# Four of seven w_down operands with their low part by DMA, and a later start of VectorE's larger planned cost

## The chip, the cores and the metric

The kernel runs on one core of a Trainium2 chip. The metric is the device time of one execution in microseconds (us), lower is better; the time of a version is the median of several runs. Engines: TensorE (PE, with PEld for its weight loads), VectorE (DVE), ScalarE (ACT), GpSimd (POOL) and SyncE (SP), which issues most of the DMAs.

## The reference, cut to what matters

One step of a hybrid decoder layer for 1032 tokens (1024 prompt and 8 sample tokens), width 1024, in float32. The part that matters here is the end of the layer:

```python
x = x + cross_attn(rmsnorm(x, g_attn), mk, mv, w_q, w_o)
h = rmsnorm(x, g_ffn)
x = x + (jax.nn.silu(h @ w_gate) * (h @ w_up)) @ w_down     # D_FF = 2816
y = rmsnorm(x, g_final)
```

## The kernel before

**Precision.** Every float32 operand of a product is split into a high part (float32 rounded to TensorE's float32r format, written by a copy) and a low part (the operand minus its high part). A product is three passes, high by high, high by low and low by high (`PASSES`, line 53). Two helpers make the parts. `split` (line 338) has the high part written by ScalarE or GpSimd and the low part by a subtraction on VectorE or GpSimd. `split_by_dma` (line 363) has ScalarE write the high part (line 368), then minus the high part into the low part's place (line 368 again, `hb<-hb`), and then GpSimd's queue issues a DMA that adds the raw operand from DRAM to it (line 375, `hb<-hb`, an accumulating DMA).

**The gate and up products.** 22 tiles of 128 hidden columns, in a Strassen-like scheme with seven products a tile (`of_tokens`, `product` at line 1273, matmuls at line 1290) in place of eight; VectorE adds the products from PSUM into `su` (line 1305), VectorE or GpSimd multiply by the row factor `Rf` (line 1331), ScalarE takes the silu (line 1338). The weights of a tile are added up (line 1249) and split (lines 346 to 357) into `wG`, `wU`, `wTa`, `wTb` while the tile before runs. The first 16 tiles leave their hidden values, already combined to seven operands, in DRAM (`hb`), in four chunks of 512 rows of w_down; the last six go through `hd` and the stage after.

**The w_down products.** 4 chunks of 4 units (`down(u)`, chunk c = u // 4), each of seven products (`A11, S2, A12, S3, S1, A22, S4`, the order of `DOWN_ORDER`, line 57). A unit's weights are loaded (`dn_load`, `dr`), added up (`dn_prep`, line 1431, `dt`) and split into `dW` and `dV`, one unit ahead. The chunk's seven operands are loaded by SP (`down_blocks`, tile `hs`) and split into `hb` tiles: chunk 0 by `split`, chunks 1 to 3 by `split_by_dma` (line 1449). They are asked for during the chunk before, two in its second unit, two in its third and three (S1, A22, S4) in its fourth. In chunk 0 four results of a unit go out of PSUM by ScalarE (line 1309), all the others by VectorE (line 1305). After the 16 units `last_down` (line 1587) takes the last six tiles, and the final norm follows.

**The order of the work.** Nothing is ordered by hand here. `Program.add` notes each piece of work with its planned cost on every engine that may take it, its reads and its writes; `Program.order` then plans all pieces at once, always the one that can start first, with small slacks and a priority by place in the program, and emits the instructions in that order. So the planned costs decide which engine gets a piece and in which order each engine's queue runs; the chip then runs each queue in order. VectorE's planned cost is `dve(n) = fixed["DVE"] + 0.00105 * n`, with a fixed part of 0.065 at the start of the program and 0.148 from the attention output projection on (line 1512). It is read when a piece is noted. In the plan GpSimd does not start while a VectorE piece marked `lock` runs, nor the other way round; on the chip no wait between the two is emitted for that. Tiles come from small pools: 19 of the big operand tiles (`op`), 3 `scr` (among them `hs`), 3 `raw` (`dr`, `dt`), and in PSUM `mm` and `ms`, which hold three products at a time.

Of the kernel before, what the change touches and what calls it, by code (L numbers as in the profile page):

```python
# [66 lines left out]
DOWN_ORDER = (A11, S2, A12, S3, S1, A22, S4)  # L67
# [175 lines left out]
def hybrid_step_kernel(ctx: ExitStack, tc: tile.TileContext, io):  # L243
# [11 lines left out]
    def buf(name, tag, shape, dtype=F32):  # L255
        return Buf(name, tag, shape, dtype)
# [4 lines left out]
    def op_r(name, shape=(P, 2, T)):  # L261
        return buf(name, "op", shape, F32R)

    def scr(name, shape=(P, T)):
        return buf(name, "scr", shape)
# [20 lines left out]
    fixed = {"DVE": 0.065}  # L286
# [47 lines left out]
    def dma(out, in_, nbytes, r=(), w=()):  # L334

        add({"SP": 0.05}, lambda e: e.dma_start(out(), in_()), r, w, nbytes=nbytes)

    def split(dst, key, src, n, r, gain=None, ps=False):

        hi = {"ACT": act(n, ps, gain is not None)}  # L340
        if not ps:
            hi["Pool"] = pool_ts(n)

        def emit_hi(e):
            if e is nc.scalar:
                e.activation(dst(0), src(), AF.Copy, scale=1.0 if gain is None else gain)
            else:
                e.tensor_scalar(dst(0), src(), 1.0 if gain is None else gain, 1.0, ALU.mult, ALU.mult)

        add(hi, emit_hi, r, [key(0)])  # L350
        lo = {"DVE": dve(n)}
        if gain is None and not ps:
            lo["Pool"] = pool_tt(n)

        def emit_lo(e):
            if gain is None:
                e.tensor_tensor(dst(1), src(), f32(dst(0)), ALU.subtract)  # L357
            else:
                e.scalar_tensor_tensor(dst(1), src(), gain, f32(dst(0)), ALU.mult, ALU.subtract)

        add(lo, emit_lo, list(r) + [key(0)], [key(1)], lock=not ps)

    def split_by_dma(dst, key, src, n, r, again, again_keys, pool_too=False):


        def scaled(e, p, src, factor):
            if e is nc.scalar:
                e.activation(dst(p), src, AF.Copy, scale=factor)  # L368
            else:
                e.tensor_scalar(dst(p), src, factor, 1.0, ALU.mult, ALU.mult)  # L370

        either = {"ACT": act(n), "Pool": pool_ts(n)} if pool_too else {"ACT": act(n)}
        add(either, lambda e: scaled(e, 0, src(), 1.0), r, [key(0)])
        add(either, lambda e: scaled(e, 1, f32(dst(0)), -1.0), [key(0)], [key(1)])
        add({"Pool": 1.04}, lambda e: e.dma_start(dst(1), again(), accum_op=ALU.add), [key(1)] + again_keys, [key(1)], nbytes=4 * P * n)
# [848 lines left out]
    def gu_load(f):  # L1224
        gu_raw[f] = [buf(f"gr{f}_{i}", "raw", (P, D)) for i in range(2)]
        for i, raw in enumerate(gu_raw[f]):
            dma(lambda raw=raw: raw[:], lambda i=i: io["w_gu"][2 * f + i], 4 * P * D, w=[(raw,)])
# [4 lines left out]
    def gate_prep(f):  # L1232
        rg, _ = gu_raw[f]
        gu_w[f] = [buf(f"wG{f}", "w", (P, 2, 1024), F32R)]
        parts(gu_w[f][0], lambda: rg[:], 1024, [(rg,)])

    def sums_prep(f):
        rg, ru = gu_raw.pop(f)
        U = buf(f"wU{f}", "w", (P, 2, 512), F32R)
        Ta, Tb = op_r(f"wTa{f}", (P, 2, 1024)), op_r(f"wTb{f}", (P, 2, 1024))  # L1240
        ta, tb = scr(f"ta{f}", (P, 1024)), scr(f"tb{f}", (P, 1024))
        gu_w[f] += U, Ta, Tb
        lo, hi = slice(0, 512), slice(512, 1024)

        def minus(dst, sl, a, asl, b, bsl, op=ALU.subtract):
            def key(t, s):
                return (t,) if t in (rg, ru) else (t, s.start)

            add({"Pool": pool_tt(512), "DVE": dve(512)}, lambda e: e.tensor_tensor(dst[:, sl], a[:, asl], b[:, bsl], op),
                [key(a, asl), key(b, bsl)], [key(dst, sl)], lock=True)  # L1250

        minus(tb, lo, ru, lo, rg, lo)
        minus(ta, lo, tb, lo, ru, hi)
        minus(ta, hi, ru, hi, ru, lo)
        minus(tb, hi, rg, hi, ta, lo, ALU.add)
        parts(Ta, lambda: ta[:], 1024, [(ta, 0), (ta, 512)])
        parts(Tb, lambda: tb[:], 1024, [(tb, 0), (tb, 512)])
        parts(U, lambda: ru[:, hi], 512, [(ru,)])
# [97 lines left out]
    def first_two(f, between=lambda: None):  # L1356
        G = gu_w[f][0]
        su[f] = op_buf(f"su{f}", (P, 4, TH))
        copy_sums(part(f, 1), (su[f], 1), of_tokens(G, 0, A11, 4 if f < AHEAD else 1))
        between()  # L1360
        plus(f, 1, 0, of_tokens(G, 512, A12, 4 if f < AHEAD else 1))
        gated(f, 0)

    def sixth(f):
        plus(f, 1, 2, of_tokens(gu_w[f][2], 0, S2, 4 if not f else 1))
# [30 lines left out]
    def later(work, bias="prep"):  # L1396
        pg.later = BIAS[bias]
        work()
        pg.later = 0
# [15 lines left out]
    def dn_load(u):  # L1415
        dn_raw[u] = buf(f"dr{u}", "raw", (P, D))
        dma(lambda: dn_raw[u][:], lambda: io["w_dn"][u], 4 * P * D, w=[(dn_raw[u],)])

    def dn_prep(u):
        raw, t = dn_raw[u], buf(f"dt{u}", "raw", (P, D))  # L1420
        W, V = buf(f"dW{u}", "w", (P, 2, 768), F32R), op_r(f"dV{u}", (P, 2, 1024))
        dn_w[u] = W, V

        def b(half, i):
            return lambda: raw[:].rearrange("p (k i n) -> p k i n", k=4, i=2)[:, half::2, i]

        def s(q):
            return lambda: t[:].rearrange("p (q j n) -> p q j n", q=4, j=2)[:, q]

        def minus(q, a, b, keys, op=ALU.subtract):  # L1430
            add({"Pool": pool_tt(256), "DVE": dve(256)}, lambda e: e.tensor_tensor(s(q)(), a(), b(), op), keys, [(t, q)], lock=True)

        minus(0, b(0, 1), b(0, 0), [(raw,)])
        minus(2, s(0), b(1, 1), [(raw,), (t, 0)])
        minus(3, b(1, 1), b(0, 1), [(raw,)])
        minus(1, b(1, 0), s(2), [(raw,), (t, 2)], ALU.add)
        split(lambda p: V[:, p], lambda p: (V, p), lambda: t[:], 1024, [(t, q) for q in range(4)])
        split(lambda p: W[:, p, :512].rearrange("p (k n) -> p k n", k=4), lambda p: (W, p, 0),
              lambda: raw[:].rearrange("p (k i n) -> p k i n", k=4, i=2)[:, :, 0], 512, [(raw,)])
        split(lambda p: W[:, p, 512:].rearrange("p (k n) -> p k n", k=2), lambda p: (W, p, 1), b(1, 1), 256, [(raw,)])  # L1440

    def down_blocks(c, which):
        for b in which:
            t = scr(f"hs{c}_{b}", (P, 2, TH))
            dma(lambda t=t: t[:], lambda b=b: hb[c, b], 8 * P * TH, r=[("hb", c, b, j) for j in range(2)], w=[(t,)])
            o = db[c, b] = op_r(f"hb{c}_{b}", (P, 2, 2, TH))
            part, key, src = (lambda p, o=o: o[:, p]), (lambda p, o=o: (o, p)), (lambda t=t: t[:])
            if c:
                split_by_dma(part, key, src, T, [(t,)], lambda b=b: hb[c, b], [("hb", c, b, j) for j in range(2)])
            else:  # L1450
                split(part, key, src, T, [(t,)])
# [57 lines left out]
        hops.append(ho)  # L1509


    fixed["DVE"] = 0.148
    for n in O_ORDER:
        proj_o(n)
        j, i = n % 4, n // 4
# [14 lines left out]
    for f in range(FF_TILES):  # L1530
        if f + 1 < FF_TILES:
            if f + 1 >= AHEAD:
                later(lambda: gu_load(f + 1), "load")
                later(lambda: gate_prep(f + 1))
            later(lambda: sums_prep(f + 1))
        else:
            later(lambda: dn_load(0), "load")
            later(lambda: dn_prep(0))
            later(lambda: down_blocks(0, DOWN_ORDER[:4]))
        if f < AHEAD:  # L1540
            sixth(f)
        else:
            first_two(f, lambda: sixth(f))
        others(f)
    later(lambda: down_blocks(0, DOWN_ORDER[4:]))
    units = 4 * CHUNKS
    for u in range(units):
        c, p = u // 4, u % 4
# [191 lines left out]
```

## Time and profile before

| | before |
|---|---|
| median of 3 runs | 1266.01 us (1265.66 to 1266.23) |
| the profiled execution | 1266.04 us, of it span 1264.2 us |
| busy: PE, PEld | 1218.6 us (96%), 1196.0 us (95%) |
| busy: DVE, ACT, POOL | 909.9 us (72%), 531.8 us (42%), 497.8 us (39%) |
| mean granted TensorE clock | 0.991 |
| gate and up products | 556.43 to 1010.48 us of the span |
| w_down products, 16 units | 1010.48 to 1182.26 us |
| last six tiles, final norm | 1182.26 us to the end |

An engine's row in the timeline gives the start, the time and the count of merged instructions; the bracket behind it is the idle time of the engine just before and what ended it. The chain of waits follows the work that ended last back through what released each step. Below, "stall" is idle time of TensorE.

### The profile page before, as it was taken

What the parts mean: (1) busy time and instruction counts of PE and PEld (TensorE: products, weight loads), DVE (VectorE), ACT (ScalarE), POOL (GpSimd) and SP (SyncE); (2) the same over time, 40 slices, a digit from 0 to 9 for tenths busy, and PEclk for the clock granted to TensorE, in tenths of its full rate; (3) what the DMA queues carried; (4) which work ended last, traced back from release to release, by engine and by line L of the source; (5) the groups of instructions that cost most, each with busy time, mean ns of one, the idle gap of its engine ahead of it and who ended that gap; (6) DMA issues with size and microseconds to landing.
All of it is one profiled execution on the core that took longest, in us unless ns stands there. A gap on an engine that the chain in (4) does not pass through costs nothing.

```text
span 1264.2 us, 22138 instructions
## 1 busy us (share of the span) xinstructions
PE 1218.6 (96%) x8958; PEld 1196.0 (95%) x8958; DVE 909.9 (72%) x1542; ACT 531.8 (42%) x733; POOL 497.8 (39%) x436
## 2 busy tenths in 40 slices
PE   8999997999999999999999999999999999999996
PEld 7999986999999889989999999999999989999996
DVE  7899888667367786578776868686766767766644
ACT  6766658454233443453222222222222355533544
POOL 3578741032101112125353334334433558768401
PEclk9999997999999999999999999999999999999998
DMA  7447696644265663231333133313313598889703
GB/s 278 104 83 167 144 248 171 204 106 158 89 220 198 233 259 143 85 118 59 110 101 108 61 119 109 109 60 109 118 68 118 207 297 231 215 209 246 173 23 113
DMA packets 60453, 188.62 MB, mean 149 GB/s; under 512 B 8064, under 2 KB 11840, under 8 KB 59072
## 3 DMA queue, kind: packets, MB, share of 16 engines
q1 hardware_dynamic: 52288, 157.74, 35.3%
q0 software_dynamic: 8064, 29.47, 13.1%
q8 instruction: 70, 1.15, 0.4%
q14 instruction: 31, 0.25, 0.1%
HBM read 153.55 MB, written 33.64 MB: 148 GB/s over the span
## 4 chain that ended last, share of the span: by engine, by line
PE 73%; DVE 8%; issue 7%; DMA 6%; ACT 3%; POOL 2%; SPq 0%; DVEq 0%; POOLq 0%; ACTq 0%
PE pr L1290 41%; PE ps L457 12%; PE fd L1587 5%; PE oa L457 4%; PE ob L457 4%; DVE cacc L663 2%; DMA dr<-in_w_dn 2%; PE sc L1000 2%; PE pv L1058 2%; DMA raw<-in_w_v 2%; DVE su L1331 1%; DMA hb<-hb 1%; POOL w L357 1%; ACT hb L368 1%; PE psg L457 1%
## 5 line engine op out<-in xcount | busy, mean ns | idle before, releaser
L1305 DVE TENSOR_TENSOR su<-pr,su 128x258 f32<-128x258 f32 (+1 forms) x204 | 109.5, 558 | 98.2 <-PE pr L1290 91.6
L1290 PE MATMUL pr<-ab,wG 128*128 128x258 f32 x1056 | 134.8, 284 | 6.1 <-DVE su L1305 3.8
L1290 PEld LDWEIGHTS pr<-ab,wG 128*128 128x128 f32 x1056 | 129.9, 189 | 7.8 <-DVE su L1305 4.4
L1290 PE MATMUL pr<-ab,wTa 128*128 128x258 f32 x1056 | 134.1, 283 | 0.0
L1290 PE MATMUL pr<-ab,wTb 128*128 128x258 f32 x1056 | 130.5, 283 | 0.0
L1290 PEld LDWEIGHTS pr<-ab,wTa 128*128 128x128 f32 x1056 | 130.0, 189 | 0.0
L1290 PEld LDWEIGHTS pr<-ab,wTb 128*128 128x128 f32 x1056 | 128.5, 189 | 0.0
L457 PE MATMUL ps<-xop,w 128*128 128x344 f32 x720 | 114.1, 320 | 0.6 <-DMA w<-in_w_in 0.6
L457 PEld LDWEIGHTS ps<-xop,w 128*128 128x128 f32 x720 | 113.3, 188 | 0.9 <-DMA w<-in_w_in 0.9
L1290 PE MATMUL pr<-hb,dV 128*128 128x258 f32 x768 | 99.5, 286 | 3.1 <-ACT x L1309 2.1
L1290 PEld LDWEIGHTS pr<-hb,dV 128*128 128x128 f32 x768 | 96.0, 192 | 3.9 <-ACT x L1309 2.4
L457 PE MATMUL ps<-xq,w 128*128 128x344 f32 x576 | 94.8, 321 | 0.0
L457 PE MATMUL po<-oo,w 128*128 128x344 f32 x576 | 91.0, 320 | 0.4 <-DVE oo L1063 0.4
L457 PEld LDWEIGHTS po<-oo,w 128*128 128x128 f32 x576 | 90.7, 188 | 0.7 <-DVE oo L1063 0.7
L457 PEld LDWEIGHTS ps<-xq,w 128*128 128x128 f32 x576 | 90.6, 188 | 0.1
L1305 DVE TENSOR_TENSOR x<-pr,x 128x258 f32<-128x258 f32 (+1 forms) x122 | 63.7, 556 | 28.8 <-PE pr L1290 25.7
L1290 PE MATMUL pr<-hb,dW 128*128 128x258 f32 x576 | 75.6, 284 | 3.9 <-DMA hb<-hb 2.5
L663 DVE SCALAR_TENSOR_TENSOR cacc<-glu,vec,cacc 128x511 f32<-128x511 f32 (+14 forms) x116 | 77.0, 741 | 0.0
L1290 PEld LDWEIGHTS pr<-hb,dW 128*128 128x128 f32 x576 | 71.7, 189 | 5.1 <-DMA hb<-hb 3.2
L1331 DVE TENSOR_TENSOR su<-su,Rf 128x516 f32<-128x516 f32 x66 | 64.6, 981 | 10.8 <-ACT su L1338 10.4
L1587 PE MATMUL fd<-ho,w 128*128 128x258 f32 x576 | 70.0, 283 | 0.0
L1587 PEld LDWEIGHTS fd<-ho,w 128*128 128x128 f32 x576 | 69.4, 189 | 0.1
(319 smaller groups left out, 2330.2 us busy)
## 6 DMA issues: line engine op xcount, KB each, us to landing
gr<-in_w_gu SPq DMA_DIRECT2D x44, 512.0 KB, 3.4
hs<-hb SPq DMA_DIRECT2D x28, 516.0 KB, 6.9
hb<-hb POOLq DMA_DIRECT2D x21, 516.0 KB, 9.2
hb<-su SPq DMA_DIRECT2D x8, 1032.0 KB, 4.5
dr<-in_w_dn SPq DMA_DIRECT2D x16, 512.0 KB, 8.8
spcache_k<-in_cache_k SPq DMA_DIRECT2D x12, 512.0 KB, 4.7
raw<-in_w_in SPq DMA_DIRECT2D x10, 512.0 KB, 5.3
w<-in_w_in POOLq DMA_DIRECT2D x9, 512.0 KB, 6.8
```

What stands on the lines that cost most here:

```text
L357: e.tensor_tensor(dst(1), src(), f32(dst(0)), ALU.subtract)
L368: e.activation(dst(p), src, AF.Copy, scale=factor)
L457: e.matmul(ps[:, c, :CW], w[:, wi, cols], x[:, xi, c * CW : (c + 1) * CW], start=first and p == 0, stop=last and p == 2)
L663: e.scalar_tensor_tensor(acc[h][:, n:], src[:, : HALF - n], w, acc[h][:, n:], ALU.mult, ALU.add)
L1000: e.matmul(bank()[:, i * NMEM : (i + 1) * NMEM], qop[2 * h + dt][:, qi, tt * P : (tt + 1) * P], kk[:, ki, 2 * (h % 2) + dt], start=(dt == ...
L1058: e.matmul(ps[:, c], v[:, vi, m, col : col + P], pT[h][m][:, pi, sl], start=(m == 0 and p == 0), stop=(m == 1 and p == 2))
L1290: e.matmul(bank(c), w[:, wi, cols(j)], xs[0](j, xi)[:, c * TQ : (c + 1) * TQ], start=j == 0 and p == 0, stop=j == nj - 1 and p == 2)
L1305: from_sums(sums, "DVE", dve, lambda e, src, sl: e.tensor_tensor(as_banks(o(sl), src), src, as_banks(a(sl), src), ALU.add), [akey], [okey])
L1331: add({"Pool": pool_tt(TH), "DVE": dve(TH)}, lambda e: e.tensor_tensor(o(), o(), b(), ALU.mult), r + [(su[f], q)], [(su[f], q)], lock=True)
L1587: e.matmul(view(i), w[:, wi, col : col + P], hops[k][:, xi, lo + i * width // count : lo + (i + 1) * width // count], start=(k == 0 and p ...
```

## The change

Two edits. In `down_blocks`, chunks 1 to 3 keep `split_by_dma` for the first four operands (A11, S2, A12, S3); S1, A22 and S4 go through `split`, as all seven of chunk 0 do. The statement that raises the fixed part of VectorE's planned cost from 0.065 to 0.148 moves from before the attention output projection to the last gate-and-up tile, just ahead of the first `dn_load`. Pieces noted between the two places (the output projection, its splits and norm, the weights of all 22 tiles and the products of tiles 0 to 20) are now planned with 0.065; no instruction of theirs changes, only their place and engine may.

```diff
@@ down_blocks
-            if c:
+            if c and b in DOWN_ORDER[:4]:
                 split_by_dma(part, key, src, T, [(t,)], lambda b=b: hb[c, b], [("hb", c, b, j) for j in range(2)])
             else:
                 split(part, key, src, T, [(t,)])
@@ ahead of the output projection
-    fixed["DVE"] = 0.148
     for n in O_ORDER:
         proj_o(n)
@@ the loop over the 22 tiles, branch of the last tile
         else:
+            fixed["DVE"] = 0.148
             later(lambda: dn_load(0), "load")
             later(lambda: dn_prep(0))
             later(lambda: down_blocks(0, DOWN_ORDER[:4]))
```

## Rows read from the trace of the kernel before

**Rows 1.** The page, busy time of the engines over the whole span.

```profile
PE 1218.6 (96%) x8958; PEld 1196.0 (95%) x8958; DVE 909.9 (72%) x1542; ACT 531.8 (42%) x733; POOL 497.8 (39%) x436
```

**Rows 2.** Busy time by stretch: the output projection; two stretches of the gate and up products; the four chunks of the w_down products. Columns: stretch, its length, PE, PEld, DVE, ACT, POOL busy (with counts), granted TensorE clock, DMA share, GB/s.

```profile
480.00:556.00 76.00, 75.61 (x481) 75.33 (x479) 48.34 (x54) 32.14 (x41) 11.05 (x6) 1.00 0.29 105
...
661.48:784.22 122.74, 121.44 (x1011) 121.23 (x1009) 89.02 (x125) 30.66 (x41) 48.79 (x32) 1.00 0.28 98
...
906.94:1010.48 103.54, 101.40 (x842) 101.01 (x841) 70.59 (x99) 26.77 (x37) 39.70 (x27) 1.00 0.35 126
...
1010.48:1056.80 46.32, 42.99 (x336) 42.07 (x337) 33.10 (x59) 28.66 (x38) 29.79 (x25) 0.96 0.87 259
1056.80:1097.63 40.83, 40.80 (x339) 40.59 (x338) 28.12 (x50) 19.41 (x23) 30.08 (x32) 1.00 0.90 233
1097.63:1140.69 43.06, 41.04 (x339) 40.63 (x338) 27.23 (x50) 18.87 (x22) 32.14 (x34) 1.00 0.86 223
1140.69:1182.26 41.57, 40.88 (x339) 40.62 (x337) 30.03 (x53) 16.98 (x20) 35.03 (x30) 1.00 0.89 225
```

**Rows 3.** Waits of TensorE (who waited for whom: total us, times, longest), from 556 to 1011 us.

```profile
PE pr L1290 <- DVE su L1305: 4.7, 4, 1.3
PE pr L1290 <- POOL wG L357: 1.3, 1, 1.3
PE pr L1290 <- ACT wU L346: 0.8, 1, 0.8
```

**Rows 4.** Timeline of TensorE at the stalls of the w_down products.

```profile
1010.48 1.68 PE L1290 MATMUL pr<-hb,dW 128*128 128x258 f32 x12 [0.90 <-DVE su L1305]
...
1037.93 1.86 PE L1290 MATMUL pr<-hb,dV 128*128 128x258 f32 x12 [2.15 <-ACT x L1309]
...
1050.92 4.61 PE L1290 MATMUL pr<-hb,dV 128*128 128x258 f32 x36 [0.79 <-DVE x L1305]
...
1106.30 0.40 PE L1290 MATMUL pr<-hb,dW 128*128 128x258 f32 x2
1108.55 2.90 PE L1290 MATMUL pr<-hb,dW 128*128 128x258 f32 x22 [1.85 <-DMA hb<-hb]
...
1150.56 2.92 PE L1290 MATMUL pr<-hb,dW 128*128 128x258 f32 x22 [0.69 <-DMA hb<-hb]
```

**Rows 5.** The chain of waits, three DMAs on it and what came behind the second (start us, us, what).

```profile
1023.77 12.60 DMA dr<-in_w_dn
...
1102.35 8.69 DMA dr<-in_w_dn
...
1111.13 1.26 DVE dt L1431
...
1138.79 11.73 DMA hb<-hb
```

**Rows 6.** The `hb` operands over the whole span, by line and engine (ns: least, median, most; first and last start).

```profile
L368 ACT ACTIVATE hb<-hs x21: 1050/1068/1073, 1015.5 to 1136.3; 128x1032 fp32r<-128x1032 f32 x21
L368 ACT ACTIVATE hb<-hb x21: 1062/1072/1074, 1017.0 to 1137.4; 128x1032 fp32r<-128x1032 f32 x21
L375 POOL DMA_DIRECT2D hb<-hb x21: 852/876/1174, 1018.4 to 1138.8; - x21
...
L357 POOL TENSOR_TENSOR hb<-hs,hb x4: 2410/2584/2779, 993.6 to 1012.2; 128x1032 fp32r<-128x1032 f32 x4
L357 DVE TENSOR_TENSOR hb<-hs,hb x3: 1219/1234/3493, 994.0 to 1007.7; 128x1032 fp32r<-128x1032 f32 x3
```

**Rows 7.** DMA from 1006 to 1182 us: the queue of GpSimd's DMAs (packets, MB, share of the 16 engines), and issues by operand with KB each and median us to landing; then SP's own waits from 950 to 1190 us.

```profile
q0 software_dynamic: 3785, 13.91, 42.6%
...
hb<-hb POOLq DMA_DIRECT2D x21, 516.0 KB, 9.2
...
SPq L336 <- ACT hb L368: 62.6, 20, 9.9
```

**Rows 8.** Timelines of ScalarE at the stalls of 1108 us, 1050 us and 1150 us, and of VectorE ahead of the one at 1010 us.

```profile
1093.28 1.05 ACT L368 ACTIVATE hb<-hs 128x1032 fp32r<-128x1032 f32 x1
...
1050.44 1.07 ACT L368 ACTIVATE hb<-hb 128x1032 fp32r<-128x1032 f32 x1
1051.41 0.58 ACT L1309 ACTIVATE x<-pr 128x516 f32<-128x516 f32 x1
...
1136.34 1.05 ACT L368 ACTIVATE hb<-hs 128x1032 fp32r<-128x1032 f32 x1
...
1007.70 1.23 DVE L357 TENSOR_TENSOR hb<-hs,hb 128x1032 fp32r<-128x1032 f32 x1 [0.61 <-ACT hb L346]
```

**Rows 9.** Groups of VectorE's instructions from 664 to 908 us, shapes apart (count, busy us, mean ns, idle before).

```profile
L1305 DVE TENSOR_TENSOR su<-pr,su 128x516 f32<-128x516 f32 x55 | 38.1, 692 | 43.5 <-PE pr L1290 43.2
L1331 DVE TENSOR_TENSOR su<-su,Rf 128x516 f32<-128x516 f32 x36 | 37.3, 1036 | 5.4 <-ACT su L1338 5.1
```

**Rows 10.** Timelines of VectorE, GpSimd and TensorE round one stall of the gate and up products.

```profile
782.62 2.74 DVE L1331 TENSOR_TENSOR su<-su,Rf 128x516 f32<-128x516 f32 x1
...
782.41 2.40 POOL L357 TENSOR_TENSOR wTa<-ta,wTa 128x1024 fp32r<-128x1024 f32 x1
...
785.76 3.03 PE L1290 MATMUL pr<-ab,wG 128*128 128x258 f32 x23 [1.26 <-DVE su L1305]
```

**Rows 11.** Busy time and clock behind the stall at 1037 us, columns as in rows 2.

```profile
1036.00:1042.00 6.00, 3.90 (x21) 3.60 (x22) 3.31 (x8) 3.09 (x5) 3.10 (x2) 0.78 0.91 279
```

## The prediction

> **What bounds the kernel now.** First the page: TensorE is busy 1218.6 of 1264.2 us, its weight loads 1196.0 [rows 1]. The change removes no matmul, so only stalls of TensorE (and a lowered clock) can go or come. Second, busy time by stretch, to see where the stalls lie [rows 2]. The output projection has almost none (75.61 of 76.00 us busy). The gate and up products lose 1.30 us in 122.74, and 2.14 in the last 103.54. The four w_down chunks do the same matmuls in 46.32, 40.83, 43.06 and 41.57 us: the second is the measure of an undisturbed chunk, so the other three lose 5.49, 2.23 and 0.74 us, 8.46 together. Third, TensorE's waits: from 556 to 1011 us VectorE's evacuations cost 4.7 us in 4 stalls, weights at the start 1.3 and 0.8 [rows 3]. The timeline of the w_down products names the rest: 0.90, 2.15, 0.79, 1.85 and 0.69 us [rows 4]. So all that can be gained from the two edits is some 4.7 + 2.1 + 8.5 = 15.3 us; what a bad order can cost has no such bound.
>
> **Part 1: nine operands split by engines in place of DMA.** Removed, for each of nine: one ScalarE pass of 1.07 us (minus the high part), one GpSimd issue of 0.88 us and one accumulating DMA, 9.2 us in the median from issue to landing [rows 6, 7]. Added: one subtraction, 1.23 us on VectorE or 2.58 on GpSimd, and the high part may go to GpSimd too [rows 6].
>
> Gain a: the two stalls on `hb<-hb`, 1.85 + 0.69 = 2.54 us [rows 4]. Which operand is it? From a chunk's first unit, products come in the order A11, S2, A12, S3, S1, A22, S4; the stalled group of 24 is S4 of the first unit with the next A11. Two of its matmuls ran, on the high part, and the third, the first that reads the low part, waited. S4 is one of the three that change. Its high part was begun at 1093.28 us in chunk 2 and at 1136.34 in chunk 3 [rows 8]; the DMA of chunk 3 was issued at 1138.79 and landed 11.73 us later [rows 5]. By an engine the low part would be there 1.07 + 2.58 = 3.65 us after the high part began if it ran at once: by about 1097 and 1140, against uses at 1106 and 1150. Some 9 us are left for queueing, so I count both stalls as gone.
>
> The Trainium skill ("DMA: Bandwidth & Descriptors", Anatomy of one DMA) speaks against this gain: such a DMA takes 2.0 us plus bytes over 436,000 per us, which for 528,384 bytes is an estimate of 3.2 us. By that the low part of chunk 3 would have landed at 1142, no wait would stand in the trace, and the gain would be 0. The row says 11.73 us [rows 5], and the row decides.
>
> What is late next: in chunk 2 VectorE's queue stood at the additions for the next unit until a weight load, issued at 1102.35, landed 8.69 us later; it moved on at 1111.13 [rows 5], after the 1108.55 at which TensorE's stall ended. If that load is no earlier, TensorE fills its three PSUM places and stops there instead, and most of the 1.85 comes back. I take it that the load comes earlier: GpSimd's DMAs hold the 16 engines for 42.6% of this stretch [rows 7], 27 of them (21 `hb` and six `ho`, of near one size), so nine fewer free about 14% of it, three of them issued between 1091 and 1096 us, just ahead of that load. Kept for the range: 1.85 lost again.
>
> Gain b: 0.79 us at 1050.92 [rows 4]. PSUM was full because ScalarE's copy of a result came only at 1051.41, behind the passes for chunk 1's S1 and A22, of which one ended at 1051.4 [rows 8]. Two of these four passes go: 2 x 1.07 us, more than the stall.
>
> Cost c: nine subtractions. At VectorE's 1.23 us they are 11.1 us on top of 118.5 busy in 171.8 us [rows 2]: room as a sum, but each can stand ahead of an evacuation. The new wait is VectorE's (or GpSimd's) for the high part; behind it on VectorE stand evacuations, and for them TensorE. The nearest rows are chunk 0, whose seven operands are split this way: one waited 0.61 us for ScalarE, took 1.23, and TensorE lost 0.90 right after [rows 8, 4]. That is 0.13 us an operand, 1.2 us for nine. Bounds: 0 (all covered by the 53 us that VectorE is idle), and nine times the 0.90, 8.1 us. I take 1.2, as chunk 0 is the same operation. SP pays too: an `hs` place now comes free after the low part, not after the high one, so loads behind it wait up to 2.58 us longer on a queue that already waits 62.6 us for such passes [rows 7]; covered by the 9 us above, uncovered it is inside the 8.1.
>
> Untouched: the 2.15 us at 1037.93, where ScalarE stood behind a weight load of 12.60 us issued at 1023.77 [rows 4, 5]. Chunk 1's first four operands, whose DMAs run beside it, stay by DMA. The 6 us behind it ran at a granted clock of 0.78 [rows 11], a mean between the two levels of 1.2 and 2.4 GHz, after TensorE had been idle; about 0.22 x 6 = 1.3 us more. If the new order moves that load, up to 3.5 us are gained; if the load slips further, as much is lost. I take 0.
>
> **Part 2: the plan's fixed part, 0.065 in place of 0.148 for the output projection and 21 tiles.** The instructions stay; the order may change everywhere from there. Planned times fall by 0.083 us an instruction. The larger value is the accurate one: 0.148 + 0.00105 x 516 = 0.690 us, measured 0.692 [rows 9]; with 0.065 the plan says 0.607. With 125 VectorE instructions in six tiles [rows 2] the plan falls 10.4 us short in 122.7. That is no time by itself: VectorE waits 43 us in 244 for TensorE in one group alone [rows 9], and three products fit in PSUM, some 8 us of matmuls. It matters through the order between VectorE and GpSimd, which the plan fixes and the chip doesn't enforce. The stall at 785 us shows how: GpSimd began a 2.40 us subtraction at 782.41, VectorE a product with `Rf` at 782.62; that took 2.74 us until GpSimd was done, the evacuation behind it was late and TensorE lost 1.26 [rows 10]. Call it a lost race. They are common (such a product takes 1036 ns in the mean, 692 being normal for its size [rows 9]) but only one in six tiles reaches TensorE, 3 in 21 tiles of the 4 stalls in [rows 3]. I take the same count after: cost 0, bounds minus 3.8 (all three gone) and plus 8.9 (two more in each of 3.5 stretches of six tiles, 7 x 1.27).
>
> **Sum of the forecast.** 1266.04 (profiled execution, 1.8 us outside its span; it stands 0.03 above the median, so no correction) - 2.54 - 0.79 + 1.2 = 1263.9 us. Its own spread, with the load that may be late (+1.85) and the cost c from 0 to 2.4, is 1262.7 to 1267.
>
> **The rivals.**
> - *Slower: more lost races.* A plan that takes VectorE for faster than it is lets GpSimd's long subtractions start first more often. For it: the plan is now 12% short there, and 1.27 us a time is seen. Against: most such waits are absorbed already. One more in six tiles gives 1263.9 + 3.5 x 1.27 = 1268.3; from that rate on it is slower by over 0.2%; two more give 1272.8. The Trainium skill ("SBUF — State Buffer", Who interferes with whom) has the same mechanism, an exclusive lock that goes to whichever starts first; the rows at 782 us agree.
> - *Faster: the races fall the other way.* A cheaper VectorE also draws work from GpSimd, whose 2.4 us pieces do the blocking, to VectorE. All three stalls gone: 1263.9 - 3.8 = 1260.1; with the 2.1 us at the start as well, 1258.0.
> - *The gain is hidden anyway.* The weight load stays late, cost c takes the rest, and the reordering comes to nothing: 1263.9 + 1.85 = 1265.8, up to 1267.
>
> **How the numbers follow.** A measurement of this kernel tells about 0.2% (2.5 us) from no change, so faster is under 1263.5 and slower over 1268.5. Forecast 0.40, half of it on either side of 1263.5; slower rival 0.25; faster rival 0.22; hidden 0.13. Faster: 0.20 + 0.22 = 0.42. Same: 0.20 + 0.13 = 0.33. Slower: 0.25. The range leaves out the far ends of both rivals: 1257.5 to 1271.
>
> **What would show it.** Right: no wait of TensorE on `hb<-hb`, chunks 2 and 3 near 40.9 us, the stall at 1051 gone, 12 accumulating DMAs of `hb`. Part 2: the stalls on line 1305 between 586 and 1010 us still three, with VectorE products on line 1331 of over 2 us ahead of them. Wrong: stalls on VectorE in the last unit of a chunk (cost c too small), a weight load again over 8 us near 1105, or a new stall in every sixth tile or oftener, or in the output projection, which now has none.

## The result, and the profile after

The changed kernel takes 1253.58 us, the median of 5 runs (1253.05 to 1255.75), against 1266.01 (1265.60 to 1268.69) for the kernel before beside it: ratio 0.9903, interval 0.9888 to 0.9917. The profiled execution took 1254.77 us with a span of 1252.9, 11.3 less than the span before. The forecast was 1263.9, its range 1257.5 to 1271: the time fell below the range.

The page's first part and the windows by stage, columns as in [rows 1, 2]. The stages after begin at other times than before, so each window has its own limits: the output projection, the gate and up products in five pieces, and the four chunks of w_down.

```profile
PE 1215.9 (97%) x8958; PEld 1194.3 (95%) x8958; DVE 926.7 (74%) x1564; ACT 529.7 (42%) x731; POOL 458.8 (37%) x407
```

```profile
482.00:558.04 76.04, 75.21 (x479) 74.97 (x477) 47.43 (x53) 32.82 (x42) 14.24 (x9) 1.00 0.30 105
558.04:587.91 29.87, 28.61 (x222) 26.98 (x223) 27.82 (x37) 17.34 (x25) 10.23 (x9) 1.00 0.27 89
587.91:663.00 75.09, 75.09 (x624) 75.09 (x625) 58.35 (x87) 20.00 (x26) 30.76 (x19) 1.00 0.29 99
663.00:785.00 122.00, 122.00 (x1017) 122.00 (x1016) 91.78 (x132) 32.35 (x44) 36.41 (x23) 1.00 0.28 98
...
908.00:1006.27 98.27, 98.27 (x821) 98.27 (x819) 72.32 (x96) 27.01 (x37) 36.52 (x24) 1.00 0.38 138
```

```profile
1006.27:1049.20 42.93, 41.57 (x338) 40.77 (x337) 33.66 (x56) 25.81 (x36) 30.06 (x26) 1.00 0.94 271
1049.20:1089.70 40.50, 40.50 (x339) 40.50 (x338) 29.71 (x52) 14.73 (x19) 33.12 (x28) 1.00 0.68 179
1089.70:1130.15 40.45, 40.45 (x339) 40.45 (x338) 31.27 (x51) 17.66 (x21) 31.49 (x30) 1.00 0.74 197
1130.15:1170.89 40.74, 40.74 (x338) 40.64 (x337) 33.15 (x57) 17.45 (x20) 33.19 (x29) 1.00 0.84 206
```

Read the second column against the length. From 587.91 to 1006.27 us, and again from 1049.20 to 1170.89, the two are equal: TensorE is not idle at all. Before, the same stretches lost 1.30 and 2.14 us in two pieces and 2.02 and 0.69 in chunks 2 and 3 [rows 2].

| stage, us | before | after | difference |
|---|---|---|---|
| up to the first output product | 464.65 | 466.25 | +1.6 |
| output projection to the first gate product | 91.78 | 91.79 | 0.0 |
| gate and up products | 454.05 | 448.23 | -5.8 |
| w_down, chunks 0 and 1 | 87.15 | 83.43 | -3.7 |
| w_down, chunks 2 and 3 | 84.63 | 81.20 | -3.4 |
| behind them | 81.94 | 82.01 | +0.1 |

The first line is not the change's: kernels with the same instructions up to there began the output projection anywhere from 460 to 466 us. The rest gives -12.9 us of stages, in three parts. Of these the forecast had the last, and 0.8 us of the second.

TensorE's waits in the gate and up products (556 to 1007 us; before in [rows 3]), then its timeline at every stall of the w_down products (before in [rows 4]):

```profile
PE pr L1290 <- ACT wU L346: 0.8, 1, 0.8
PE pr L1290 <- DVE su L1305: 0.8, 1, 0.8
PE Rf_ps L487 <- DVE Rf_m L492: 0.5, 1, 0.5
```

```profile
1012.96 1.71 PE L1290 MATMUL pr<-hb,dV 128*128 128x258 f32 x12 [0.74 <-ACT pp L1309]
1014.90 1.71 PE L1290 MATMUL pr<-hb,dW 128*128 128x258 f32 x12 [0.22 <-DVE x L1305]
...
1043.30 4.61 PE L1290 MATMUL pr<-hb,dV 128*128 128x258 f32 x36 [0.40 <-DVE x L1305]
```

An evacuation is the piece that moves a result out of PSUM. All four waits of before for VectorE's evacuations are gone (three in the tiles, and the 0.90 us at the first w_down product, which falls in the table's line of the gate and up products), and so is the wait of 1.3 us for `wG` on GpSimd. New are one of 0.81 us at 587.91 and the 0.5 us for `Rf_m`. That is 4.7 of the line's 5.8 us; the rest is busy time. Of the four later stalls of the w_down products (5.48 us) none is left as it was; three others of 1.36 us in all stand in their place. No matmul waits for `hb<-hb`.

The `hb` operands over the w_down stretch, by line and engine (before in [rows 6]), and the DMAs there (before in [rows 7]):

```profile
L368 ACT ACTIVATE hb<-hb x12: 1057/1072/1082, 1012.8 to 1109.8; 128x1032 fp32r<-128x1032 f32 x12
L375 POOL DMA_DIRECT2D hb<-hb x12: 844/878/1200, 1019.3 to 1112.8; - x12
L357 POOL TENSOR_TENSOR hb<-hs,hb x9: 2409/2425/3276, 991.3 to 1125.4; 128x1032 fp32r<-128x1032 f32 x9
L357 DVE TENSOR_TENSOR hb<-hs,hb x7: 1228/1817/2845, 990.8 to 1126.6; 128x1032 fp32r<-128x1032 f32 x7
```

```profile
q0 software_dynamic: 2543, 9.38, 30.5%
...
hb<-hb POOLq DMA_DIRECT2D x12, 516.0 KB, 7.8
```

So nine accumulating DMAs went, as the change says, GpSimd's DMAs hold the 16 engines for 30.5% in place of 42.6%, and of the nine new subtractions five are GpSimd's (9 against 4) and four VectorE's (7 against 3). They last longer on VectorE than the 1.23 us of the forecast: the median of all seven is 1.82.

### The profile page after: what moved, and what is told of

Read it like the earlier page. It is cut to its first block, busy times and chain, and to the rows that moved or that the text cites. A ratio compares the mean times of both kernels' runs of the same rounds, so it can differ in the third digit from the quotient of the medians.

```text
span 1252.9 us, 22090 instructions
## 1 busy us (share of the span) xinstructions
PE 1215.9 (97%) x8958; PEld 1194.3 (95%) x8958; DVE 926.7 (74%) x1564; ACT 529.7 (42%) x731; POOL 458.8 (37%) x407
## 4 chain that ended last, share of the span: by engine, by line
PE 73%; DVE 10%; issue 7%; DMA 5%; ACT 2%; POOL 2%; SPq 0%; DVEq 0%; POOLq 0%; ACTq 0%
PE pr L1290 45%; PE ps L457 11%; PE fd L1587 6%; PE oa L457 4%; PE ob L457 4%; DVE cacc L663 2%; DMA raw<-in_w_v 2%; PE sc L1000 1%; DVE spcache_v L1097 1%; DMA spcache_k<-in_cache_k 1%; POOL w L357 1%; PE pv L1058 1%; DVE spcache_k L1097 1%; DMA w<-in_w_in 1%; DVE xss L384 1%
## 5 line engine op out<-in xcount | busy, mean ns | idle before, releaser
L1305 DVE TENSOR_TENSOR su<-pr,su 128x258 f32<-128x258 f32 (+1 forms) x204 | 109.3, 558 | 71.0 <-PE pr L1290 69.9
L1305 DVE TENSOR_TENSOR x<-pr,x 128x516 f32<-128x516 f32 (+1 forms) x122 | 63.3, 556 | 23.2 <-PE pr L1290 22.0
L346 ACT ACTIVATE w<-raw 128x1024 fp32r<-128x1024 f32 (+2 forms) x34 | 31.6, 932 | 90.2 <-issue 38.2
```

What stands on the lines that cost most here:

```text
L1305: from_sums(sums, "DVE", dve, lambda e, src, sl: e.tensor_tensor(as_banks(o(sl), src), src, as_banks(a(sl), src), ALU.add), [akey], [okey])
```

## The experiments

Names for what follows: *split* is the first edit (four of seven by DMA), *plan* the second (0.065 for the output projection and the tiles). Ratios are to the kernel before, timed beside each kernel. "Tiles" is the time of the gate and up products, "chunks" that of the w_down products, both in us of the profiled execution. Theories to be told apart: of the tiles, that they gain by which GpSimd subtractions stand beside which VectorE products, or by the plan's being nearer to or further from the measured times; of the w_down chunks, that the split alone gains there, or only together with the plan.

**1. The split alone (e1_split_only).**

```diff
-            if c:
+            if c and b in DOWN_ORDER[:4]:
```

> The split edit alone, the planned cost as in the kernel before. Theory A (each edit works in its own stage): the tiles stay as before, 454.1 us with three stalls of 1.3 us on VectorE's evacuations, and the w_down units fall from 171.8 to about 164.6 us as in the changed kernel: 1266.0 - 7.2 = 1258.8 us. Theory B (the stall behind the late weight load at 1037 us went because the moved statement left another order there): only the two waits on the accumulating DMA and the 0.8 us on ScalarE go, the 2.15 us stall with its lowered clock stays: w_down units about 168.5 us, 1262.7 us.

Measured: 1265.01 us, ratio 0.9981 (0.9965 to 0.9998), slower than either theory had it. Tiles 453.7; chunks 2 and 3 40.56 and 40.79; but chunks 0 and 1 89.83, 2.7 more than before and 6.4 more than after. So the split gives 3.3 us in chunks 2 and 3 and takes 2.7 from the first two. TensorE's two stalls, VectorE and GpSimd at them, and the load that was late again (start, us, what):

```profile
1050.98 1.72 PE L1290 MATMUL pr<-hb,dV 128*128 128x258 f32 x12 [0.69 <-ACT pp L1309]
1055.12 2.95 PE L1290 MATMUL pr<-hb,dW 128*128 128x258 f32 x12 [2.41 <-DVE x L1305]
```

```profile
1049.55 4.57 DVE L357 TENSOR_TENSOR hb<-hs,hb 128x1032 fp32r<-128x1032 f32 x2
1054.05 1.95 DVE L1305 TENSOR_TENSOR x<-pr,x 128x258 f32<-128x258 f32 x4
```

```profile
1050.51 2.52 POOL L357 TENSOR_TENSOR hb<-hs,hb 128x1032 fp32r<-128x1032 f32 x1 [2.55 <-ACT hb L346]
```

```profile
1031.46 11.95 DMA dr<-in_w_dn
```

VectorE has two `hb` subtractions in a row. GpSimd begins a third at 1050.51 and holds it until 1053.03; VectorE's pair takes 4.57 us in place of twice 1.23, the four evacuations behind it start at 1054.05, and TensorE has stood for 2.41. This is cost c of the prediction, an estimated 3.9 us of it with the clock (a mean of 0.73 from 1052.5 to 1058: 0.27 x 5.5 = 1.5 us).

**2. The plan alone (e2_fixed_only).** The kernel after, with `if c:` again.

> The moved planned cost alone, all seven operands of chunks 1 to 3 by DMA as before. Theory A: the tiles take 448.2 us with no stall of the kind in the kernel before, the attention part is 1.6 us longer, the w_down units keep their 171.8 us with waits on the accumulating DMA: 1266.0 - 5.8 + 1.6 = 1261.8 us. Theory B: the w_down units fall too, by the 3.5 us of the late weight load: 1258.3 us.

Measured: 1263.96 us, ratio 0.9976 (0.9963 to 0.9989), again slower than either theory had it. Tiles 447.58: the whole gain there is the plan's. Chunks 0 and 1 89.1, chunks 2 and 3 43.1 and 43.3, with 1.95 and 2.30 us on `hb<-hb` in their first units. Chunks 0 and 1 apart:

```profile
1005.18:1048.45 43.27, 41.58 (x339) 40.75 (x338) 33.61 (x55) 28.85 (x40) 30.46 (x26) 1.00 0.96 268
1048.45:1094.27 45.82, 42.83 (x338) 42.21 (x337) 27.65 (x51) 19.43 (x23) 28.94 (x33) 0.96 0.79 209
```

The plan alone brings chunk 0 from 46.32 [rows 2] to 43.27 us, near the 42.93 of after, and chunk 1 from 40.83 up to 45.82. There a weight load issued at 1051.08 landed 13.00 us later and TensorE lost 2.69 to it. The two edits alone gave 0.19% and 0.24%, together 0.97%: they don't add.

**3. The plan for the tiles alone (e3_tiles_only).** After, with 0.148 for the output projection.

```diff
+    fixed["DVE"] = 0.148
     for n in O_ORDER:
         proj_o(n)
...
+    fixed["DVE"] = 0.065
     rsqrt_rows("Rf", Rf, RF, xss2
```

> The changed kernel with VectorE's fixed part at 0.148 for the output projection as before, and 0.065 for the norm of the rows and the tiles alone. If the 1.6 us that the changed kernel lost ahead of the output projection come from planning the projection's weight splits with 0.065, and the tiles' gain from planning the tiles with it: 1253.6 - 1.6 = 1252.0 us. If the tiles' gain hangs on the order in which the projection leaves the queues, the three stalls of 1.3 us come back: about 1256 us.

Measured: 1252.24 us, ratio 0.9877 (0.9861 to 0.9893), tiles 447.35, chunks 83.5, 40.45 and 40.75. The output projection has no part in it.

**4. Before, with the tile weights' low parts on VectorE only (e4_low_on_vector).**

```diff
-        split(lambda p: w[:, p], lambda p: (w, p), src, n, r)
+        split(lambda p: w[:, p], lambda p: (w, p), src, n, r, lo_pool=False)
```

(`lo_pool=False` takes the choice of GpSimd from the planner.)

> The kernel before, both edits undone, but the low parts of the tile weights (wG, wU, wTa, wTb) may be subtracted on VectorE only, no longer on GpSimd. If the stalls in the tiles come from GpSimd's subtractions of 2.4 us that begin just ahead of a VectorE piece with two inputs in SBUF: no stall of over 1 us on line 1305's evacuations between tiles, tiles 454.1 - 3.8 = 450.3 us or less, 1262.2 us. Rival, that an accurate plan matters and VectorE simply has too much to do: VectorE gets about 13 us more work in 122, and the stalls stay or grow: 1266 us or more.

Measured: 1265.01 us, ratio 0.9979 (0.9968 to 0.9991). Tiles 448.7, with the old 0.148: the three stalls of 1.24 to 1.30 us are gone by taking away GpSimd's long subtractions, though the plan still believes 0.148 of VectorE. (The w_down products took 173.63, 1.85 more than before, so the total shows less.) VectorE's `Rf` products from 664 to 908 us in before, after and here stand in this order; the first is in [rows 9]:

```profile
L1331 DVE TENSOR_TENSOR su<-su,Rf 128x516 f32<-128x516 f32 x39 | 29.3, 750 | 4.9 <-ACT su L1338 4.4
```

```profile
L1331 DVE TENSOR_TENSOR su<-su,Rf 128x516 f32<-128x516 f32 x41 | 30.7, 749 | 0.5
```

Mean 1036, 750 and 749 ns. The products that wait for GpSimd are what went.

**5. 0.107 for the tiles, 0.148 for the output projection (e8_tiles_0107)**: e3 with the value between.

> The run with 0.148 for the output projection, but 0.107 in place of 0.065 for the tiles, halfway. If a smaller planned cost works by drawing long subtractions from GpSimd to VectorE, the count of such pieces on GpSimd between 664 and 908 us lies between 20 (0.148) and 12 (0.065), and the tiles take 447.4 to 454 us, with one stall or none in six tiles: 1252 to 1256 us. If the value acts by chance, through the order alone, the tiles can also take longer than 454 us.

Measured: 1251.88 us, ratio 0.9899 (0.9875 to 0.9922), tiles 447.0, chunks 83.57, 40.45, 40.82. The row of its `Rf` products, and GpSimd's long subtractions there in before, in this kernel and in after:

```profile
L1331 DVE TENSOR_TENSOR su<-su,Rf 128x516 f32<-128x516 f32 x36 | 25.3, 704 | 1.0 <-ACT su L1338 0.5
```

```profile
L357 POOL TENSOR_TENSOR wTb<-tb,wTb 128x1024 fp32r<-128x1024 f32 x6 | 14.4, 2395 | 33.6 <-ACT wTb L346 33.4
L357 POOL TENSOR_TENSOR wTa<-ta,wTa 128x1024 fp32r<-128x1024 f32 x4 | 9.6, 2400 | 0.0
L357 POOL TENSOR_TENSOR wG<-gr,wG 128x1024 fp32r<-128x1024 f32 x4 | 9.6, 2399 | 7.8 <-ACT wG L346 7.8
```

```profile
L357 POOL TENSOR_TENSOR wTb<-tb,wTb 128x1024 fp32r<-128x1024 f32 x6 | 14.4, 2402 | 34.5 <-ACT wTb L346 34.5
L357 POOL TENSOR_TENSOR wTa<-ta,wTa 128x1024 fp32r<-128x1024 f32 x4 | 9.7, 2412 | 0.0
```

```profile
L357 POOL TENSOR_TENSOR wTa<-ta,wTa 128x1024 fp32r<-128x1024 f32 x4 | 9.6, 2411 | 6.0 <-ACT wTa L346 6.0
L357 POOL TENSOR_TENSOR wTb<-tb,wTb 128x1024 fp32r<-128x1024 f32 x4 | 9.6, 2394 | 32.3 <-ACT wTb L346 32.3
L357 POOL TENSOR_TENSOR wG<-gr,wG 128x1024 fp32r<-128x1024 f32 x2 | 4.8, 2395 | 21.5 <-ACT wG L346 21.5
```

Of 14 pieces of 2.4 us ten are left in both. In the kernel with 0.107 GpSimd is still busy 94.7 us in this stretch (97.6 before, 73.2 after), and yet it has the shortest products and no such stall. So it is not GpSimd's load that decides, but which piece starts just ahead of a product. The traces of all 18 kernels bear this out: each of their 196 `Rf` products of over 1 us began while a piece of GpSimd's was running, and ended 0.54 to 0.56 us after that piece. In before 17 of 66 products are such, in the kernel with 0.107 five of 66.

**6. 0.023 for the tiles (e12_tiles_0023).**

> 0.148 for the output projection, 0.023 for the tiles, as far below 0.065 as 0.107 is above it. If any smaller planned cost keeps the lost races away: tiles 447.4 us, Rf products of 0.7 to 0.75 us in the mean, 1252 us. If the value acts by chance, through the order alone: stalls come back, and products of over 2 us ahead of them; or the plan, now 18% short, is late everywhere and the tiles exceed 450 us: 1255 us or more.

Measured: 1264.47 us, ratio 0.9978 (0.9962 to 0.9995). Tiles 451.05, products of 816 ns: worse again, so less is not always better. (From 664 to 908 us TensorE has no stall; those of 0.69, 0.98 and 1.95 us are at 594, 642 and 1008 us.) In w_down a load of `x` went among four accumulating DMAs (issued in pairs at 1021.76 and 1024.72 us). Chunks 0 and 1 took 87.7, with a stall of 3.39 us behind this (start, us, what of the chain):

```profile
1025.53 15.70 DMA x<-x2d
```

**7 and 8. Which chunks' split gives what (e5_chunk1_split, e6_chunks23_split).** Both are the kernel after; the first goes back to seven DMAs in chunks 2 and 3, the second in chunk 1.

```diff
-            if c and b in DOWN_ORDER[:4]:
+            if c and (b in DOWN_ORDER[:4] or c > 1):     # e5
+            if c and (b in DOWN_ORDER[:4] or c == 1):    # e6
```

> The changed kernel, but S1, A22 and S4 go by engines in chunk 1 only; chunks 2 and 3 take all seven by DMA again. Theory C: a chunk's loss is set by how many accumulating DMAs stand ahead of a weight load, chunk by chunk, so chunks 0 and 1 keep their 42.9 and 40.5 us, and chunks 2 and 3 go back to 43.1 and 43.3 as in the run with the moved statement alone: 1253.6 + 2.7 + 2.5 = 1258.8 us. Theory D (the gain of the two together is a lucky order of the whole end): any other pattern, chunks 0 and 1 changed as well.

> The counterpart: S1, A22 and S4 by engines in chunks 2 and 3, chunk 1 all seven by DMA. Theory C: the four accumulating DMAs between 1041 and 1051 us return and with them the weight load of 13 us and the stall of 2.7 us in chunk 1 with its lowered clock: chunks 0 and 1 together 89 us against 83.4, chunks 2 and 3 at 40.5 and 40.8: 1253.6 + 5.7 = 1259.3 us. Theory D: no stall of that kind, or one elsewhere.

Measured: e5 1256.87 us, ratio 0.9929 (0.9910 to 0.9949), chunks 0 and 1 83.6, then 42.6 and 41.9, where the waits on `hb<-hb` are back (1.46 and 0.94 us). e6 1257.50, ratio 0.9932 (0.9910 to 0.9953), chunks 0 and 1 87.07, then 40.5 and 40.8. So about 3.6 us hang on chunk 1's three operands and 3.3 on the others' six. How chunk 1's three do it, in e6: GpSimd's accumulating DMAs, the chain behind them, and TensorE.

```profile
1037.96 0.88 POOL L375 DMA_DIRECT2D hb<-hb  x1 [1.41 <-ACT hb L368]
...
1040.01 0.87 POOL L375 DMA_DIRECT2D hb<-hb  x1 [0.40 <-ACT hb L368]
...
1042.55 0.88 POOL L375 DMA_DIRECT2D hb<-hb  x1 [0.90 <-ACT hb L368]
...
1047.23 0.87 POOL L375 DMA_DIRECT2D hb<-hb  x1
```

```profile
1047.45 12.94 DMA dr<-in_w_dn
...
1060.48 0.42 DVE dt L1431
1060.91 0.35 DVE x L1305
```

```profile
1061.30 1.93 PE L1290 MATMUL pr<-hb,dW 128*128 128x258 f32 x12 [2.72 <-DVE x L1305]
```

Four accumulating DMAs in 10 us, then a weight load of 512 KB that takes 12.94 us. VectorE stands at the addition for it, the evacuations are queued behind, PSUM fills up. After, the accumulating DMAs of this time go out singly or in a pair (at 1019.28, 1023.35 and two from 1032.75 us), and those weight loads from 1002 to 1066 us whose landing the trace shows took 4.8 to 8.9 us.

**9 to 11. The late load without the plan (e7_chunk1_no_dma, e9_chunks23_plan_before, e10_ask_later).** All three are the kernel before. e7 has no DMA of `hb` in chunk 1 and four of seven in chunks 2 and 3; e9 has seven in chunk 1 and four in the others; e10 keeps all and asks for chunk 1's first four one unit later.

```diff
+            if c > 1 and b in DOWN_ORDER[:4]:            # e7
+            if c and (b in DOWN_ORDER[:4] or c == 1):    # e9
-    ((), DOWN_ORDER[:2], DOWN_ORDER[2:4], DOWN_ORDER[4:])[p]
+    ((), DOWN_ORDER[:2] if c else (),
+     DOWN_ORDER[2:4] if c else DOWN_ORDER[:4], DOWN_ORDER[4:])[p]    # e10
```

> Planned cost as before, chunk 1 with no operand by DMA, chunks 2 and 3 with the first four. If the weight load of 12 us and the stall at 1037 us come from the four accumulating DMAs issued beside it (chunk 1's first four), the load lands in about 6 us and chunks 0 and 1 take some 83.5 us in place of 87.1 (before) and 89.8 (split edit alone): 1265.0 - 6 = 1259 us. If the load is late because it is issued late, it stays at 10 us or more and chunk 0 stays above 45 us; four more subtractions of 1.23 us then make it slower: 1265 us or more.

> The split edit in chunks 2 and 3 only, planned cost as before, so that chunk 1's last three stay by DMA. If the split edit alone gains nothing because its subtractions for chunk 1 (4.57 us for two on VectorE at 1050 us) cost in chunk 0 what chunks 2 and 3 give: chunks 0 and 1 stay at 87.1 us, chunks 2 and 3 take 40.6 and 40.8 in place of 43.1 and 41.6: 3.3 us under the kernel before. Rival, that nothing adds up because the plan of the whole end changes: chunks 0 and 1 off by more than 1.5 us, the sum anywhere.

> The kernel before, both edits undone, with chunk 1's first four operands asked for one unit later in chunk 0 (none in its second unit, four in its third). If the stall at 1037 us comes from accumulating DMAs that run beside the weight load of that unit, the load issued near 1024 us lands in 4 to 7 us in place of 12.6, the 2.15 us stall and its lowered clock go, and chunk 0 takes 43 to 44 us: about 1263 us. If the load is late by its issue alone, the stall stays near 2 us: 1266 us. The four DMAs may instead delay a load of the next unit: then the same stall one unit later.

Measured: e7 1267.74 us, ratio 1.0012 (0.9998 to 1.0025): the loads land in 4.7 us in the median from 1005 to 1090 (10.6 before), so the accumulating DMAs do make them late; but chunks 0 and 1 take 92.0, since two short additions of VectorE (`dt`, 0.41 us otherwise) stand beside one of GpSimd's `hb` subtractions (2.87 us from 1022.31) and an addition of its behind that (1.46 us from 1025.14), and take 4.05 us from 1022.83; with the six pieces after them, an `hb` subtraction among these, no evacuation runs until 1030.69, and TensorE loses 6.08. e9 1262.56, ratio 0.9965 (0.9950 to 0.9980): chunks 2 and 3 give 3.3 us, chunks 0 and 1 take 88.1 with a load of 12.81. e10 1271.29, ratio 1.0031 (1.0016 to 1.0046), a loss: the same late load (11.46 us, issued at 1029.30) came one unit later, with stalls of 2.05, 1.05 and 3.14 us.

**12. Three of seven by DMA (e11_three_by_dma)**: e8 with `DOWN_ORDER[:3]`.

> The run with 0.107 for the tiles, and three of seven operands by DMA in place of four (S3 by engines too). If accumulating DMAs still cost: chunks 0 to 3 fall below 164.8 us by up to 1.5: 1250.5 us. If the subtractions are by now the dearer side: a stall behind one of 1.23 to 2.6 us, chunk 0 or 1 longer by 1 to 4 us: 1253 to 1256 us.

Measured: 1255.41 us, ratio 0.9909 (0.9888 to 0.9930). Chunks 0 and 1 88.7, with e1's pair of subtractions again: 4.57 us from 1040.12 beside GpSimd's 2.51 from 1041.09, and 2.13 us lost. One DMA fewer is no gain where the subtraction lands badly.

**13 and 14. Is e1's loss the pair of subtractions? (e13_split_low_gpsimd, e14_split_low_vector).** e1 with the low parts of chunks 1 to 3 on one engine only, GpSimd or VectorE. (Three lines more, so L1308 is L1305.)

```diff
+        if lo_only:
+            lo = {lo_only: lo[lo_only]}
...
-                split(part, key, src, T, [(t,)])
+                split(part, key, src, T, [(t,)], lo_only="Pool" if c else None)   # e14: "DVE"
```

> The split edit alone, planned cost as before, and the low parts of chunks 1 to 3 (nine) on GpSimd only. If the stall of 2.41 us at 1055 us with its lowered clock comes from VectorE's second subtraction waiting for GpSimd's with evacuations queued behind it: no such stall, chunks 0 and 1 near 85.5 us in place of 89.8, 1261 us. If instead the weight load of 12 us or ScalarE's high parts set it, the stall stays; GpSimd's queue, 2.4 us longer for each, may also hold up the weights' additions: 1265 us or more.

> As the run before, but the nine low parts on VectorE only. No subtraction of an operand can then be held up by another on GpSimd: two of them take 2.5 us in place of 4.57, so the 2.41 us stall falls under 0.5 and chunks 0 and 1 take 86 to 87 us: 1262 us. If VectorE is simply too full in that burst, three in a row (3.7 us) stop the evacuations as long as before: 1265 us.

Measured: e13 1262.50 us, ratio 0.9962 (0.9942 to 0.9981), chunks 0 and 1 86.5 in place of 89.83. e14 1266.49, ratio 0.9992 (0.9979 to 1.0005), a miss, chunks 0 and 1 86.9: the 2.41 us became 0.65, but chunk 3 got a new stall.

```profile
1051.68 1.71 PE L1293 MATMUL pr<-hb,dW 128*128 128x258 f32 x12 [0.65 <-DVE x L1308]
...
1165.77 5.95 PE L1293 MATMUL pr<-hb,dV 128*128 128x258 f32 x36 [2.76 <-DVE x L1308]
```

So some 3 us of e1's loss go with this pair. In e13 the 2.41 us is gone, but the weight load was issued behind the bunch again (12.15 us, at 1032.22), and then VectorE's `dV` subtraction took 3.46 us from 1048.91 beside GpSimd's three of `hb` (8.28 us from 1048.89); TensorE lost 1.49, 1.63 and 0.55. How the 3 us still missing to 83.4 divide between the two is not shown.

**15 and 16. The best found (e15_three_low_gpsimd, e16_0107_low_gpsimd).** e11 and e8, with the low parts of chunks 1 to 3 on GpSimd.

> The run with three by DMA and 0.107 for the tiles (1255.4 us, with the stall of 2.13 us at 1045 us), low parts of chunks 1 to 3 on GpSimd only. If that stall is the same one: it goes, chunks 0 and 1 from 88.7 to 84 us, 1251 us. If not: 1255 us or more.

> The run with four by DMA and 0.107 for the tiles (1251.9 us, where the two subtractions on VectorE have four evacuations between them and no such stall stands), low parts of chunks 1 to 3 on GpSimd only. There is nothing of that kind to gain: 1251 to 1252.5 us if the order holds; longer by 2 to 5 us if the changed order of GpSimd makes a weight late.

Measured: e15 1255.50 us, ratio 0.9913 (0.9884 to 0.9941); the four chunks take 168.65 (85.2 and 83.5 by pairs), two stalls of 1.45 and 1.61 us are left: a miss. e16 1249.97 us (4 runs), ratio 0.9874 (0.9837 to 0.9910), tiles 447.08, chunks 83.35, 40.49, 40.94. By stage it equals e8; its profiled execution, the shortest, reached the output projection at 460.00 us, which varies from run to run. e3, e8 and e16 all beat the kernel before by 1.0 to 1.3%; their intervals overlap with that of after, so none is shown to beat it, though all three medians are lower.

## Why the prediction failed

**The reading of the bound held.** Only stalls and the clock could move, and 12.9 of the 15.3 us that the prediction counted as all there was to gain were gained. The error is in how much of it was expected.

**Gain a held in mechanism, too small in size.** 2.54 us were forecast, 3.4 came. Every run with engines for the last three operands in chunks 2 and 3 took 81.2 to 81.7 us there, with two exceptions, e14 (87.0) and e15 (83.5), where VectorE's evacuations were late; every run without took 84.5 or more. The question of what is late next was answered rightly: the stall did not move to the weight load. The estimate of 3.2 us for such a DMA, worked out from the Trainium skill ("DMA: Bandwidth & Descriptors", Anatomy of one DMA), which spoke against this gain, is not borne out here: the 12 that are left land after 7.8 us in the median.

**Gain b held by half.** 0.79 us were forecast; at the same matmul of after, at 1043.30, TensorE still waits 0.40. With all seven of chunk 1 by DMA the wait is 0.79 us in before, e2, e6, e9 and e10 (1.94 in e4); with four, and the plan at 0.065 or 0.107, it is 0.40 to 0.43 in after, e3, e5 and e8, for an evacuation of VectorE's behind an `hb` subtraction (cost c), and none in e16, where GpSimd has these subtractions. The reading was loose too: the row names VectorE as what ended the wait at 1050.92, and ScalarE's copy at 1051.41 began after that [rows 4, 8].

**Cost c was mis-sized as a constant.** 1.2 us were taken, 0.13 an operand. It is near nothing in chunks 2 and 3 and 0.40 us in after as a whole, but some 3.9 in e1 and 6 or more in e7. It depends on what VectorE does beside GpSimd's subtraction, and on how many pieces stand ahead of the next evacuation: in e1 a pair of subtractions, in e7 eight pieces. After has both pieces too, but with four evacuations between them:

```profile
1041.33 1.23 DVE L357 TENSOR_TENSOR hb<-hs,hb 128x1032 fp32r<-128x1032 f32 x1
1042.47 1.96 DVE L1305 TENSOR_TENSOR x<-pr,x 128x516 f32<-128x516 f32 x4
1044.34 1.82 DVE L357 TENSOR_TENSOR hb<-hs,hb 128x1032 fp32r<-128x1032 f32 x1
```

**"Untouched: the 2.15 us at 1037.93 ... I take 0" failed.** That stall is gone and with it the slower clock behind it. By the windows, chunk 0 is idle for 1.36 us in place of 3.33 [rows 2], and its matmuls are busy for 41.57 in place of 42.99: 2.0 + 1.4 = 3.4 us (gain b's 0.39 and a new wait of 0.74 for ScalarE are in the sum); the bounds had said "up to 3.5". The step took the load's neighbours, chunk 1's first four DMAs, to be unchanged and hence the load. They did stay by DMA, but the plan spread them: before they were issued at 1018.39, 1023.68, 1025.11 and 1027.15, after at 1019.28, 1023.35, 1032.75 and 1033.34, and the load between took 8.94 us in place of 12.60. That this is the plan's doing e2 shows, with chunk 0 at 43.27; and the same matmul waits 0.84 to 2.15 us in before, e1, e9, e10 and e14, all with the old plan, and in no run with another value for the tiles. The runs show a weight load issued among or just behind three or four accumulating DMAs landing late: 12.60 before, 11.95 in e1, 13.00 in e2, 12.94 in e6, 12.81 in e9, 11.46 in e10; with none in chunk 1 (e7) the median is 4.7. Whether a load falls there is set by the planner's order, which either edit changes.

**"I take the same count after: cost 0" failed; this is the largest error, 5.8 us.** The rival *the races fall the other way* is what happened, at more than its 3.8 us, since the waits of 1.3 us for `wG` and of 0.90 at the first w_down product went too (against 1.3 us of new ones); its 1258.0 with "the 2.1 us at the start as well" was the nearest that the prediction came. The reason given for the rival (fewer GpSimd pieces) is only half right: e4 shows that these pieces beside VectorE's products are the cause, e8 that their number is not, and e12 that a still lower value loses again. Which value gives a good order could not have been read from the trace of before; that the order was a lottery with three known losing tickets could, and a range from -3.8 to +8.9 with 0 taken leaned the wrong way.

**Adding the two parts failed.** The forecast summed them as independent. Chunks 0 and 1 take 83.3 to 83.6 us only in after, e3, e5, e8 and e16, those with the plan at 0.065 or 0.107, engines for chunk 1's three operands and four by DMA; 85.2 (e15) to 93.9 (e10) in all others. The plan spreads chunk 1's first DMAs and parts the subtractions that stopped e1; the split removes the DMAs that made the load late in e2 and e6. Neither alone does both: the plan alone gains 3.1 us in chunk 0 and loses 5.0 in chunk 1 (e2), the split alone loses in both (48.3 and 41.5 us in e1).

That the two met in a good order was luck: nothing in the prediction foresaw it, and with 0.023 for the tiles (e12) it is lost. What stays open: why the planner, with 0.065 or 0.107 in the tiles, orders chunk 1 so well. In both kernels the plan uses 0.148 from the w_down pieces on; only what the tiles leave behind differs. No run tells which of its due times tips, and e12 and e11 show how little is needed to lose it.

## What to carry to other kernels

Count the accumulating DMAs issued in the few us before each load, not only their sum over a stage: a load of half a megabyte that comes behind three or four of them is some 12 us away, and with it everything queued behind its first reader. Where VectorE and GpSimd both work on SBUF, look at which long GpSimd piece starts just ahead of a VectorE instruction that an evacuation stands behind; a planner's constant moves this by chance, so try two or three values rather than the accurate one. Two edits under one planner are to be forecast as one order, not as a sum.

## What was not expected of the hardware

Of the loads of weights and `x` from 995 us to the end of the w_down products (258 to 516 KB) whose landing the 18 traces show, the 16 that were issued while three or four accumulating DMAs of 516 KB were on their way took 11.5 to 15.7 us, and the 45 issued with none on its way 3.4 to 7.5. In the w_down stretch of after, GpSimd's queue moved 9.38 MB in 30.5% of the engines' time, SP's 27.40 MB in 49.8%: by the byte the accumulating kind holds the engines 1.8 times as long (0.305/9.38 against 0.498/27.40).

A stall of some 2 us or more is often dearer than itself. Over the 6 us behind those at 1037.93 in before (see also [rows 11]), 1055.12 in e1, 1064.98 in e2 and 1031.76 in e7 the mean granted clock was 0.72 to 0.73, between the two levels of 1.2 and 2.4 GHz. Behind 2.30 us in e2, 2.72 in e6 and 3.39 in e12 it was 1.00. What tells them apart stays open.

```profile
1052.50:1058.00 5.50, 3.09 (x15) 2.89 (x14) 3.83 (x6) 0.00 (x0) 0.53 (x1) 0.73 0.72 242
```

That row is e1's, columns as in [rows 2]: between 1052.5 and 1058 us TensorE is idle for 2.41 of 5.50, and the rest runs slower.
